# A macaron encoder block on one core: products that run on in banks filled by ScalarE, output products behind a whole group

## Chip, cores and metric

The kernel runs on one core of a Trainium2 chip. The metric is the device time of one execution in microseconds; the time of a kernel is the median of several executions. Lower is better.

## What is computed

The block takes `x` of 1024 tokens by 1024 features in float32 and applies, each with a norm in front and a residual sum behind, a half-step SwiGLU feed-forward layer, a mixing layer (a chunkwise mLSTM branch and a spatial gating branch behind one projection), and a second half-step feed-forward layer; then a last norm. All matrices are float32.

```python
def swiglu(x, w_in, w_out):                       # w_in 1024 x 5632, w_out 2816 x 1024
    gate, up = jnp.split(x @ w_in, 2, axis=-1)
    return (jax.nn.silu(gate) * up) @ w_out

x = x + 0.5 * swiglu(rmsnorm(x, ffn1_norm_g), ffn1_w_in, ffn1_w_out)
xn = rmsnorm(x, mix_norm_g)
proj = xn @ w_mix_in                              # 1024 x 8200
...                                               # mLSTM and gating branches
x = x + merged @ w_mix_out
x = x + 0.5 * swiglu(rmsnorm(x, ffn2_norm_g), ffn2_w_in, ffn2_w_out)
return rmsnorm(x, final_norm_g)
```

## The kernel before

Activations lie with features on the partitions, in two halves of 512 tokens. A float32 product is made of three products of float32r numbers: each operand is split into a rounded part (a ScalarE cast) and the rest (a VectorE subtraction), and high by high, high by low and low by high are summed in a PSUM bank of 128x512. Weights are loaded by SP into a `raw` tile (four buffers) and split into an `fw` tile (four buffers) by `unit` (L285: L287 on ScalarE, L288 on VectorE); `prod` (L291, matmul at L294) runs the products of one unit, 12 matmuls for four feature tiles, 6 for two. A framework places the instructions: each engine's queue is in order, the order comes from the framework's plan, and semaphores are set by it. Tiles of one pool are handed out in program order.

The feed-forward layer uses a scheme with seven products for a 2x2 split (gate and up columns or two output halves, two halves of the summed features, two halves of the tokens) instead of eight, with sums and differences of weights and operands.

- `first_products` (L305) runs, for all 22 feature tiles `f`, the two products of the first token half and stores two early results in DRAM (`eb`): the bank behind the first product, and the activated gate.
- `group(f)` (L321) runs the other five products for one `f`. POOL forms the weight sums (`sums`, L297: L300 to L302, and L350). The first early result is loaded into `u2` (L326). Product `t2` goes to a bank, and VectorE adds it to `u2` (L331); `t3` goes to a second bank and is added (L336); `t1` goes to a third bank `d` and is added (L341); then the function yields. Behind that the second early result is loaded (L344), `t4` is added and multiplied (L348, L349), and product `22` (L352) runs on in bank `d`, on which VectorE's L341 must have finished reading; L353 to L355 finish the gate. The hidden parts are split by `part` (L192, L193); an odd `f` forms four differences more (L365 to L371).
- `down_fast` (L381) runs the seven output products of a block of four `f` for four pairs of output tiles, with POOL's sums of 128x256 and L408, four sums from banks by VectorE (L391) and two copies by ScalarE (L397, L402) a pair; results are added to DRAM by accumulating DMAs on POOL's queue.
- `run` (L480) goes through the blocks; the output products of a block stand between the two halves of the first group of the next block. `last` (L452) finishes.

Blocks 0 to 3 have four `f` each and use `down_fast`; the last six `f` use plain output products (L430). Banks: six of `mm`, two of `ml`. The pool `t512` (11 tiles) holds `c512` tiles. In the mixing stage `feature_pair` (L148) and `token_pair` (L163) load units of four feature tiles by `load_unit` (L123). At the start eleven small DMAs on ScalarE's queue fetch parameters (L100, L104), which TensorE turns (L108) ahead of the tokens' transposes (L935).

Of the kernel before, what the change touches and what calls it, by code (L numbers as in the profile page):

```python
# [9 lines left out]
F32R = mybir.dt.float32r  # L10
# [24 lines left out]
def block_body(ctx, tc, x, ffn1_norm_g, ffn1_w_in, ffn1_w_out, mix_norm_g, w_mix_in, mlstm_conv_w,  # L35
# [31 lines left out]
    open_psum(f1, 1, mm=6, ml=2)  # L67
# [29 lines left out]
    for nm, src in (("g1", ffn1_norm_g), ("gm", mix_norm_g), ("g2", ffn2_norm_g), ("hg", mlstm_head_norm_g),  # L97
                    ("sg", sgu_norm_g), ("sb", sgu_norm_b), ("cb", mlstm_conv_b)):
        n = src.shape[-1] // P
        nc.scalar.dma_start(out=rows[at:at + n, :], in_=src[0].rearrange("(a p) -> a p", p=P))  # L100
        col[nm] = at
        at += n
    for j in range(4):
        nc.scalar.dma_start(out=rows[at:at + 16, :], in_=mlstm_conv_w[0, j].rearrange("(a p) -> a p", p=P))  # L104
# [7 lines left out]
    V.tensor_copy(out=par, in_=pt[:, 0:P])  # L112
# [10 lines left out]
    def load_unit(w_rows, ks, c0, extra=None):  # L123
# [9 lines left out]
        w = wpool[0].tile([P, 2, n, nc_], F32R, tag="w", name="w")  # L133
# [44 lines left out]
    def token_pair_wide(w_rows, c0, extra, act):  # L178
        ws = [load_unit(w_rows, ks, c0, extra) for ks in ((0, 1, 2), (3, 4, 5), (6, 7))]
# [85 lines left out]
    class Ffn:  # L265
# [31 lines left out]
        def sums(self, a11, a12, a21, a22, n):  # L297
# [23 lines left out]
        def group(self, f):  # L321
# [10 lines left out]
            w = self.unit(a21)  # L332
            b = bank("mm")
            self.prod(b, w, self.B["t3"], True, True)
            u3 = self.c512()
            V.tensor_tensor(out=u3, in0=b, in1=u2, op=ALU.add)  # L336
            w = self.unit(s1)
            d = bank("mm")
            self.prod(d, w, self.B["t1"], True, False)
            c22 = self.c512()  # L340
            V.tensor_tensor(out=c22, in0=d, in1=u3, op=ALU.add)  # L341
            yield
            sg1 = self.c512()
            nc.sync.dma_start(out=sg1, in_=self.eb[f][1])  # L344
            w = self.unit(a22)
# [28 lines left out]
            yield  # L374
# [6 lines left out]
        def down_fast(self, f0, H, acc):  # L381
            for d in range(4):
# [6 lines left out]

                def half(o, x, y):  # L390
                    V.scalar_tensor_tensor(out=o, in0=x, scalar=0.5, in1=y, op0=ALU.mult, op1=ALU.add)  # L391

# [9 lines left out]
                A.activation(out=c11, in_=a, func=AF.Copy, scale=0.5)  # L402
                G.dma_start(out=acc[0][d], in_=c11, accum_op=ALU.add)
                w = self.unit(a11, 2)
                b = bank("mm")
                self.prod(b, w, H["t2"], True, True)
                half(u2, b, u2)
                G.tensor_tensor(out=a12, in0=a12, in1=a11, op=ALU.subtract)  # L408
# [663 lines left out]
```

## Time and profile before

| | us |
|---|---|
| median of 3 runs | 2323.22 (2322.95 to 2323.43) |
| the profiled execution | 2322.64 |
| its span, first to last instruction | 2320.9 |
| TensorE busy | 2237.9 (96%) |
| VectorE busy | 1547.3 (67%) |
| ScalarE busy | 999.9 (43%) |
| GpSimd busy | 606.0 (26%) |

The profile holds one execution. PE is TensorE's matmuls, PEld its weight loads, DVE is VectorE, ACT ScalarE, POOL GpSimd, SP the engine that issues most DMAs; L294 is line 294 of the kernel. Busy is time in which an instruction ran; an engine's idle time before an instruction is put down to what ended it ("<-"). The ends of matmuls are modelled, so that a matmul is shown longer than the distance to the next one. The clock is a share of 2.4 GHz.

### The profile page before, as it was taken

How to read it: one execution, taken by the hardware profiler on the slowest of the kernel's cores; microseconds unless marked ns; L12 is line 12 of the kernel's file. 1: busy time of each engine (PE TensorE's matmuls, PEld its weight loads, DVE VectorE, ACT ScalarE, POOL GpSimd, SP SyncE). 2: the span in 40 equal slices, each digit the busy share in tenths (PEclk: the TensorE clock that was granted, in tenths of full speed). 3: DMA queues.
4: the chain of work that ended last, by engine and by line, in shares of the span. 5: the costliest groups of instructions: out<-in, count | busy, mean ns of one | idle time of the engine just before them, and what ended most of it. 6: DMA issues, size and time to landing. Idle time of an engine off the chain costs nothing. (4 is left out here: it accounts for less than half of the span.)

```text
span 2320.9 us, 30647 instructions
## 1 busy us (share of the span) xinstructions
PE 2237.9 (96%) x10979; PEld 1872.3 (81%) x10979; DVE 1547.3 (67%) x2649; ACT 999.9 (43%) x1684; POOL 606.0 (26%) x674
## 2 busy tenths in 40 slices
PE   7999999999999999999999999999999999999998
PEld 5887777777778988888889888888788777777777
DVE  6648778787467658556646575565727787877576
ACT  5633333333334345445434554543643433433333
POOL 2244545545521000000000000000215545455440
PEclk9999999999999999999999999999999999999999
DMA  8754655737753324322343353323764557366663
GB/s 264 255 176 103 142 123 124 138 106 150 159 183 123 91 81 120 100 84 81 100 146 101 89 156 91 91 82 127 251 198 145 109 136 151 93 140 126 142 181 109
DMA packets 331193, 311.52 MB, mean 134 GB/s; under 512 B 18840, under 2 KB 279576, under 8 KB 331040
## 3 DMA queue, kind: packets, MB, share of 16 engines
q1 hardware_dynamic: 292384, 217.20, 31.9%
q0 software_dynamic: 38400, 92.30, 18.7%
q8 instruction: 86, 1.41, 0.2%
q14 instruction: 67, 0.55, 0.1%
q10 hardware_dynamic: 256, 0.07, 0.0%
HBM read 223.48 MB, written 86.02 MB: 133 GB/s over the span
## 5 line engine op out<-in xcount | busy, mean ns | idle before, releaser
L294 PE MATMUL mm<-b,fw 128*128 128x512 f32 x2640 | 611.3, 392 | 23.8 <-DVE c L341 17.8
L294 PEld LDWEIGHTS mm<-b,fw 128*128 128x128 f32 x2640 | 496.2, 189 | 137.2 <-ACT fw L287 23.0
L159 PE MATMUL mm<-xn,w 128*128 128x512 f32 x2304 | 545.4, 390 | 0.0
L159 PEld LDWEIGHTS mm<-xn,w 128*128 128x128 f32 x2304 | 426.5, 188 | 82.9
L288 DVE TENSOR_TENSOR fw<-raw,fw 128x512 fp32r<-128x512 f32 (+1 forms) x472 | 325.9, 696 | 164.0 <-ACT fw L287 161.7
L294 PE MATMUL mm<-h,fw 128*128 128x512 f32 x1344 | 313.4, 393 | 21.2 <-DVE c L391 15.3
L287 ACT CAST fw<-raw 128x512 fp32r<-128x512 f32 (+1 forms) x472 | 242.3, 524 | 207.4 <-PE mm L294 133.6
L294 PEld LDWEIGHTS mm<-h,fw 128*128 128x128 f32 x1344 | 249.0, 188 | 83.9 <-issue 12.6
L135 DVE TENSOR_TENSOR w<-raw,w 128x1024 fp32r<-128x1024 f32 (+2 forms) x146 | 176.5, 1210 | 145.2 <-ACT w L134 145.0
L294 PE MATMUL mm<-xn,fw 128*128 128x512 f32 x1056 | 246.7, 395 | 4.0 <-ACT xn L192 2.1
L294 PEld LDWEIGHTS mm<-xn,fw 128*128 128x128 f32 x1056 | 199.9, 190 | 49.6 <-ACT xn L192 3.7
L134 ACT CAST w<-raw 128x1024 fp32r<-128x1024 f32 (+2 forms) x146 | 151.2, 1038 | 150.0 <-PE mm L159 82.1
L192 ACT CAST h<-c 128x512 fp32r<-128x512 f32 x136 | 82.8, 620 | 218.5 <-DVE c L349 152.1
L253 POOL DMA_DIRECT2D xs<-t x16 | 8.7, 543 | 641.4 <-DVE t L250 640.9
L300 POOL TENSOR_TENSOR s<-raw 128x512 f32<-128x512 f32 (+1 forms) x76 | 95.5, 1257 | 287.1 <-DMA raw<-in_ffn_w_in_dram 203.9
L173 PE MATMUL mm<-w,xn 128*128 128x256 f32 x1344 | 166.8, 285 | 0.2
L173 PEld LDWEIGHTS mm<-w,xn 128*128 128x128 f32 x1344 | 164.5, 193 | 1.8 <-DVE w L135 0.6
L391 DVE SCALAR_TENSOR_TENSOR c<-mm,c 128x512 f32<-128x512 f32 x160 | 110.0, 687 | 61.1 <-PE mm L294 60.8
L193 DVE TENSOR_TENSOR h<-c,h 128x512 fp32r<-128x512 f32 x136 | 100.2, 756 | 32.0 <-ACT h L192 31.6
L302 POOL TENSOR_TENSOR raw<-s,raw 128x512 f32<-128x512 f32 (+1 forms) x76 | 94.3, 1240 | 51.2 <-DVE fw L288 48.9
L448 PE MATMUL mm<-h,wl 128*128 128x512 f32 (+1 forms) x480 | 97.1, 356 | 0.0
L301 POOL TENSOR_TENSOR raw<-raw 128x512 f32<-128x512 f32 (+1 forms) x76 | 93.4, 1229 | 5.2
(244 smaller groups left out, 2548.9 us busy)
## 6 DMA issues: line engine op xcount, KB each, us to landing
raw<-in_ffn_w_in_dram SPq DMA_DIRECT2D x264, 256.0 KB, 4.2
raw<-in_w_mix_in_dram SPq DMA_DIRECT2D x124, 512.0 KB, 3.8
xd<-c POOLq DMA_DIRECT2D x160, 256.0 KB, 5.0
eb<-early POOLq DMA_DIRECT2D x88, 256.0 KB, 2.8
c<-eb SPq DMA_DIRECT2D x88, 256.0 KB, 4.6
raw<-in_ffn_w_out_dram SPq DMA_DIRECT2D x72, 256.0 KB, 3.9
xl<-xd POOLq DMA_DIRECT2D x32, 256.0 KB, 5.8
xr<-xd SPq DMA_DIRECT2D x32, 256.0 KB, 2.9
```

What stands on the lines that cost most here:

```text
L134: A.copy(out=w[:, 0, 0:n, :], in_=raw[:, 0:n, :])
L135: V.tensor_tensor(out=w[:, 1, 0:n, :], in0=raw[:, 0:n, :], in1=w[:, 0, 0:n, :].bitcast(F32), op=ALU.subtract)
L159: PE.matmul(out=banks[j], lhsT=w[:, a, i, j * P:(j + 1) * P], rhs=act[k][:, b, ts], start=(k == first and pi == 0), stop=(k == last and pi ...
L173: PE.matmul(out=o, lhsT=act[k][:, b, t * P:(t + 1) * P], rhs=w[:, a, i, :], start=(t % 2 == 0 and k == 0 and pi == 0), stop=(t % 2 == 1 an ...
L193: V.tensor_tensor(out=dst[:, 1, :], in0=src, in1=dst[:, 0, :].bitcast(F32), op=ALU.subtract)
L287: A.copy(out=w[:, 0], in_=src)
L288: V.tensor_tensor(out=w[:, 1], in0=src, in1=w[:, 0].bitcast(F32), op=ALU.subtract)
L294: PE.matmul(out=bank, lhsT=w[:, x, i, :], rhs=t[:, y, :], start=(start and i == 0 and pi == 0), stop=(stop and i == len(b) - 1 and pi == 2 ...
L300: G.tensor_tensor(out=s1, in0=a21, in1=a22, op=ALU.add)
L302: G.tensor_tensor(out=a11, in0=s1, in1=a11, op=ALU.subtract)
L391: V.scalar_tensor_tensor(out=o, in0=x, scalar=0.5, in1=y, op0=ALU.mult, op1=ALU.add)
L448: PE.matmul(out=o, lhsT=w[:, x, i, :], rhs=hs[i][:, y, ts], start=(i == 0 and pi == 0), stop=(i == n - 1 and pi == 2))
```

## The change

- In `group` the first early result is copied by ScalarE into bank `x`, in which `t2` runs on; ScalarE copies `x` into bank `y`, in which `t3` and later `t4` run on; `t1` goes to a bank of its own and is copied to `p5`. VectorE forms `y + p5` behind `t3` and `x + p5` behind `22`. The order of the products is `t2`, `t1`, `t3`, `22`, `t4`. Both early results are loaded at the group's start. The factor 0.5 goes into the hidden parts.
- `down_fast` has the same form; its weight sums are formed by VectorE instead of POOL.
- The output products of a block come behind the whole first group of the next one.
- Banks: seven of `mm`, one of `ml`. The last stage's transposes use `mm`.
- The parameter DMAs go to POOL's queue, and their transpose comes behind the tokens' (`turn_params`).
- `token_pair` loads units of three, three and two feature tiles; its split weights, and those of `token_pair_wide`, lie 16 elements into their tile.

```diff
-    open_psum(f1, 1, mm=6, ml=2)
+    open_psum(f1, 1, mm=7, ml=1)
...
-        nc.scalar.dma_start(out=rows[at:at + n, :], in_=src[0].rearrange("(a p) -> a p", p=P))
+        G.dma_start(out=rows[at:at + n, :], in_=src[0].rearrange("(a p) -> a p", p=P))
...
-    pt = psm()
-    PE.transpose(out=pt[:, 0:P], in_=rows, identity=ident)
...
+    def turn_params():
+        pt = psm()
+        PE.transpose(out=pt[:, 0:P], in_=rows, identity=ident)
+        V.tensor_copy(out=par, in_=pt[:, 0:P])
...
-        w = wpool[0].tile([P, 2, n, nc_], F32R, tag="w", name="w")
+        w = wpool[0].tile([P, 2048], F32R, tag="w", name="w")
+        w = w[:, off:off + 2 * n * nc_].rearrange("p (a k c) -> p a k c", a=2, k=n)
...
-        for u, ks in enumerate(((0, 1, 2, 3), (4, 5, 6, 7))):
-            w = load_unit(w_rows, ks, c0)
+        for u, ks in enumerate(((0, 1, 2), (3, 4, 5), (6, 7))):
+            w = load_unit(w_rows, ks, c0, off=16)
...
-            u2 = self.c512()
-            nc.sync.dma_start(out=u2, in_=self.eb[f][0])
-            s1 = self.sums(a11, a12, a21, a22, 4)
-            w = self.unit(a11)
-            b = bank("mm")
-            self.prod(b, w, self.B["t2"], True, True)
-            V.tensor_tensor(out=u2, in0=b, in1=u2, op=ALU.add)
...
-            yield
+            p1 = self.c512()
+            nc.sync.dma_start(out=p1, in_=self.eb[f][0])
             sg1 = self.c512()
             nc.sync.dma_start(out=sg1, in_=self.eb[f][1])
+            x = bank("mm")
+            A.copy(out=x, in_=p1)
+            s1 = self.sums(G, a11, a12, a21, a22, 4)
+            w = self.unit(a11)
+            self.prod(x, w, self.B["t2"], False, True)
+            y = bank("mm")
+            A.copy(out=y, in_=x)
+            w = self.unit(s1)
             b = bank("mm")
-            self.prod(b, w, self.B["t4"], True, True)
-            V.tensor_tensor(out=u3, in0=b, in1=u3, op=ALU.add)
-            V.tensor_tensor(out=u3, in0=u3, in1=sg1, op=ALU.mult)
+            self.prod(b, w, self.B["t1"], True, True)
+            p5 = self.c512()
+            A.copy(out=p5, in_=b)
+            w = self.unit(a21)
+            self.prod(y, w, self.B["t3"], False, True)
+            c22 = self.c512()
+            V.tensor_tensor(out=c22, in0=y, in1=p5, op=ALU.add)
             G.tensor_tensor(out=a12, in0=a12, in1=a11, op=ALU.subtract)
             w = self.unit(a12)
-            self.prod(d, w, self.B["22"], False, True)
-            V.tensor_tensor(out=u2, in0=d, in1=u2, op=ALU.add)
-            A.activation(out=u2, in_=u2, func=AF.Silu)
-            V.tensor_tensor(out=c22, in0=c22, in1=u2, op=ALU.mult)
+            self.prod(x, w, self.B["22"], False, True)
+            V.tensor_tensor(out=p5, in0=x, in1=p5, op=ALU.add)
+            A.activation(out=p5, in_=p5, func=AF.Silu)
+            w = self.unit(a22)
+            self.prod(y, w, self.B["t4"], False, True)
+            V.scalar_tensor_tensor(out=sg1, in0=y, scalar=0.5, in1=sg1, op0=ALU.mult, op1=ALU.mult)
+            V.scalar_tensor_tensor(out=c22, in0=c22, scalar=0.5, in1=p5, op0=ALU.mult, op1=ALU.mult)
+            u3 = sg1
...
                 w = self.unit(a11, 2)
                 a = bank("mm")
                 self.prod(a, w, H["11"], True, False)
-                u2 = self.c512()
-                A.activation(out=u2, in_=a, func=AF.Copy, scale=0.5)
-                s1 = self.sums(a11, a12, a21, a22, 2)
+                x = bank("mm")
+                A.copy(out=x, in_=a)
+                s1 = self.sums(V, a11, a12, a21, a22, 2)
+                w = self.unit(s1, 2)
+                b = bank("mm")
+                self.prod(b, w, H["t1"], True, True)
+                p5 = self.c512()
+                A.copy(out=p5, in_=b)
+                w = self.unit(a11, 2)
+                self.prod(x, w, H["t2"], False, True)
+                y = bank("mm")
+                A.copy(out=y, in_=x)
                 w = self.unit(a12, 2)
                 self.prod(a, w, H["21"], False, True)
...
                 for f in range(f0, f0 + n):
-                    g = self.group(f)
-                    next(g)
+                    self.group(f)
                     if pend is not None:
                         pend()
                         pend = None
-                    next(g)
                     spread()
...
-        bc1 = scales(0, lambda i: xt.append(turned(0, i)))
+        def step(i):
+            xt.append(turned(0, i))
+            if i == 3:
+                turn_params()
+
+        bc1 = scales(0, step)
...
-            ps = psm()
+            ps = bank("mm")
```

The rest of `down_fast` follows the same pattern: `21` in `a`, `t3` and `t4` in `y`, `22` in `x`, with VectorE's `y + p5` and `x + p5` and ScalarE's copies of `a` and the last `y`.

## Rows read from the trace of the kernel before

**Rows 1.** The page's first part: busy us, share of the span, instructions.
```profile
PE 2237.9 (96%) x10979; PEld 1872.3 (81%) x10979; DVE 1547.3 (67%) x2649; ACT 999.9 (43%) x1684; POOL 606.0 (26%) x674
```
**Rows 2.** Feed-forward stages: length, busy us of PE, PEld, DVE, ACT, POOL, clock.
```profile
153.30:661.10 507.80, 484.76 (x2090) 392.06 (x2089) 378.75 (x567) 189.32 (x372) 245.62 (x237) 0.99 0.60 133
...
1753.60:2255.70 502.10, 480.18 (x2090) 389.21 (x2088) 374.67 (x567) 189.31 (x372) 247.17 (x237) 1.00 0.60 135
```
**Rows 3.** TensorE's waits: for whom, us in total, times, longest.
```profile
PE mm L294 <- DVE c L341: 17.8, 17, 2.1
PE mm L294 <- DVE c L391: 15.3, 8, 2.1
PE mm L294 <- DVE fw L288: 7.4, 9, 1.3
PE ml L108 <- DMA raw<-in_ffn_w_in_dram: 6.5, 1, 6.5
PE mm L294 <- ACT fw L287: 6.2, 5, 1.9
```
**Rows 4.** Two groups in a row; columns as in rows 2.
```profile
266.80:280.40 13.60, 13.60 (x62) 11.26 (x61) 13.11 (x15) 4.42 (x8) 9.62 (x6) 1.00 0.63 179
280.40:295.30 14.90, 13.81 (x61) 11.15 (x60) 13.03 (x20) 6.24 (x11) 4.54 (x4) 1.00 0.27 77
```
**Rows 5.** Inside the second of them: start, us, instruction, idle time before it.
```profile
291.52 0.42 SPq L326 DMA_DIRECT2D c<-eb  x1
291.66 0.69 DVE L341 TENSOR_TENSOR c<-mm,c 128x512 f32<-128x512 f32 x1
...
292.50 4.82 PE L294 MATMUL mm<-b,fw 128*128 128x512 f32 x20 [1.08 <-DVE c L341]
...
295.65 1.62 DVE L349 TENSOR_TENSOR c<-c 128x512 f32<-128x512 f32 x1 [1.50 <-DMA c<-eb]
```
**Rows 6.** The last output pair of a block, columns as in rows 5.
```profile
252.60 3.70 DVE L288 TENSOR_TENSOR fw<-raw,fw 128x256 fp32r<-128x256 f32 x2
...
254.64 1.37 POOL L350 TENSOR_TENSOR raw<-raw 128x512 f32<-128x512 f32 x1
...
258.24 2.01 PE L294 MATMUL mm<-h,fw 128*128 128x512 f32 x6 [2.13 <-DVE c L391]
```
**Rows 7.** Groups of instructions: count, busy us, mean ns, idle before; PE whole, others first stage.
```profile
L294 PE MATMUL mm<-b,fw 128*128 128x512 f32 x2640 | 611.3, 392 | 23.8 <-DVE c L341 17.8 <-ACT fw L287 4.4 <-DVE fw L288 1.6
...
L288 DVE TENSOR_TENSOR fw<-raw,fw 128x256 fp32r<-128x256 f32 x104 | 59.5, 585 | 9.5 <-ACT fw L287 9.5
...
L336 DVE TENSOR_TENSOR c<-mm,c 128x512 f32<-128x512 f32 x22 | 15.1, 685 | 3.9 <-PE mm L294 3.9
...
L397 ACT ACTIVATE c<-mm 128x512 f32<-128x512 f32 x16 | 9.6, 597 | 12.4 <-PE mm L294 12.4
```
**Rows 8.** The page's DMA issues: count, KB each, us from issue to landing.
```profile
c<-eb SPq DMA_DIRECT2D x88, 256.0 KB, 4.6
```
**Rows 9.** Two stretches of lower clock; columns as in rows 2.
```profile
259.30:262.70 3.40, 3.40 (x10) 2.62 (x9) 1.94 (x3) 0.62 (x1) 1.73 (x2) 0.50 1.12 313
624.50:631.30 6.80, 6.20 (x13) 3.94 (x14) 6.62 (x12) 3.28 (x6) 0.00 (x0) 0.50 0.75 175
```
**Rows 10.** The start, columns as in rows 5.
```profile
8.75 0.42 ACT L903 ACTIVATE t<-xtok 128x256 f32<-128x256 f32 x1 [5.86 <-DMA t<-in_mlstm_conv_w_dram]
...
11.30 0.49 DVE L906 BATCH_NORM_STATS2 sst<-xtok 128x6 f32<-128x128 f32 x2 [0.94 <-DMA xtok<-in_x_dram]
...
25.75 24.44 PE L294 MATMUL mm<-xn,fw 128*128 128x512 f32 x94 [2.11 <-ACT xn L192]
```
**Rows 11.** Two lines: count, ns min/median/max, first and last start us.
```profile
L173 PE MATMUL mm<-w,xn x1344: 274/283/680, 727.9 to 1528.2; 128*128 128x256 f32 x192
...
L186 PE MATMUL mm<-w,xn x192: 278/285/684, 711.0 to 1217.3; 128*128 128x264 f32 x192
```
**Rows 12.** One of ScalarE's waits, columns as in rows 3.
```profile
ACT h L192 <- DVE c L349: 152.1, 44, 8.7
```

More of the change, by code (lines that the diff above doesn't have):

```diff
@@ L103, in block_body @@
     for j in range(4):
-        nc.scalar.dma_start(out=rows[at:at + 16, :], in_=mlstm_conv_w[0, j].rearrange("(a p) -> a p", p=P))
+        G.dma_start(out=rows[at:at + 16, :], in_=mlstm_conv_w[0, j].rearrange("(a p) -> a p", p=P))
         col["cw%d" % j] = at
         at += 16
-    pt = psm()
-    PE.transpose(out=pt[:, 0:P], in_=rows, identity=ident)
     par = cst.tile([P, P], F32, name="par")
@@ L111, in block_body @@
     G.memset(cpad, 0.0)
-    V.tensor_copy(out=par, in_=pt[:, 0:P])
+    def turn_params():
+        pt = psm()
+        PE.transpose(out=pt[:, 0:P], in_=rows, identity=ident)
+        V.tensor_copy(out=par, in_=pt[:, 0:P])
     def pc(nm, i):
@@ L121, in block_body, with load_unit @@
           for s in range(2)]
-    def load_unit(w_rows, ks, c0, extra=None):
+    def load_unit(w_rows, ks, c0, extra=None, off=0):
         n = len(ks)
@@ L178, in token_pair_wide @@
     def token_pair_wide(w_rows, c0, extra, act):
-        ws = [load_unit(w_rows, ks, c0, extra) for ks in ((0, 1, 2), (3, 4, 5), (6, 7))]
+        ws = [load_unit(w_rows, ks, c0, extra, 16) for ks in ((0, 1, 2), (3, 4, 5), (6, 7))]
         n = 2 * P + extra[1]
@@ L295, in prod, with sums @@
                               stop=(stop and i == len(b) - 1 and pi == 2), skip_group_check=True)
-        def sums(self, a11, a12, a21, a22, n):
+        def sums(self, G, a11, a12, a21, a22, n):
             s1 = self.sp_.tile([P, n, P], F32, tag="s", name="s")
@@ L401, in down_fast @@
                 c11 = self.c512()
-                A.activation(out=c11, in_=a, func=AF.Copy, scale=0.5)
+                A.copy(out=c11, in_=a)
                 G.dma_start(out=acc[0][d], in_=c11, accum_op=ALU.add)
[L404 to L408, printed above, removed]
-                w = self.unit(a21, 2)
-                b = bank("mm")
-                self.prod(b, w, H["t3"], True, True)
-                u3 = self.c512()
-                half(u3, b, u2)
-                w = self.unit(s1, 2)
-                e = bank("mm")
-                self.prod(e, w, H["t1"], True, False)
+                V.tensor_tensor(out=a12, in0=a12, in1=a11, op=ALU.subtract)
+                w = self.unit(a21, 2)
+                self.prod(y, w, H["t3"], False, True)
                 c22 = self.c512()
-                half(c22, e, u3)
+                V.tensor_tensor(out=c22, in0=y, in1=p5, op=ALU.add)
                 G.dma_start(out=acc[1][d + 4], in_=c22, accum_op=ALU.add)
+                w = self.unit(a12, 2)
+                self.prod(x, w, H["22"], False, True)
+                V.tensor_tensor(out=p5, in0=x, in1=p5, op=ALU.add)
+                G.dma_start(out=acc[1][d], in_=p5, accum_op=ALU.add)
                 w = self.unit(a22, 2)
-                b = bank("mm")
-                self.prod(b, w, H["t4"], True, True)
-                half(u3, b, u3)
-                G.dma_start(out=acc[0][d + 4], in_=u3, accum_op=ALU.add)
-                w = self.unit(a12, 2)
-                self.prod(e, w, H["22"], False, True)
-                half(u2, e, u2)
-                G.dma_start(out=acc[1][d], in_=u2, accum_op=ALU.add)
+                self.prod(y, w, H["t4"], False, True)
+                c21 = self.c512()
+                A.copy(out=c21, in_=y)
+                G.dma_start(out=acc[0][d + 4], in_=c21, accum_op=ALU.add)
         def down(self, f0, n, hs, acc):
@@ L439, in down @@
                         xt = self.c512()
-                        A.activation(out=xt, in_=o, func=AF.Copy, scale=0.5)
+                        A.copy(out=xt, in_=o)
                         G.dma_start(out=acc[t][d + j], in_=xt, accum_op=ALU.add)
@@ L474, in last @@
                         xt = xl[d // 2][:, d % 2, ts]
-                        V.scalar_tensor_tensor(out=xt, in0=o, scalar=0.5, in1=xt, op0=ALU.mult, op1=ALU.add)
+                        V.tensor_tensor(out=xt, in0=o, in1=xt, op=ALU.add)
                         final(t, d, part, xt)
```

24 lines of the change are left out of this document (4 added, 20 removed).

## Prediction

> **What bounds the kernel now.** I read the page's first part, then the stages, then who ends TensorE's waits, then one stretch in order of time. TensorE is busy for 96% of the span [rows 1], so only its idle time can be won, and the change keeps the number of matmuls. The two feed-forward stages hold 2090 matmuls each [rows 2]. A group without a wait has 60 of them in 13.60 us [rows 4], which is 0.2267 us apiece, so 2090 need 473.8 us. The stages took 507.8 and 502.1 us: 34.0 and 28.3 above that, 62 us together. That is the ceiling of what the feed-forward part of this change can bring.
>
> The waits name the cause. Product `22` of a group waits for VectorE's sum at L341, 17 times and 17.8 us; `22` of an output pair waits for VectorE's L391, 8 times and 15.3 us, which is once in each of the eight `down_fast`; weights that VectorE or ScalarE split late cost 7.4 and 6.2 us [rows 3]. All are products behind VectorE. A matmul is shown as 0.39 us long [rows 7] but the next follows after 0.2267, so each of these 39 waits costs 0.16 us more than shown: 46.7 + 6.4 = 53 us. Beside them the clock stood at 1.2 GHz, half, for 3.4 and 6.8 us, both times behind such a wait [rows 9]; half of 10.2 us is 5.1 us. The sum, 58, explains nearly all of the 62.
>
> Why VectorE is late is seen in [rows 4, 5]. It was busy for 13.11 us of a 13.60 us group and for 13.03 us of the next one, which took 14.90. Then it idled 1.50 us at L349 for the second early result, a DMA that SP issues late because it stands behind weight loads that themselves wait for VectorE's splits. So VectorE sets the pace there, though its share of the stage is only 379 of 508 us [rows 2].
>
> **The change part by part.**
>
> *The group.* Before, seven VectorE instructions of 128x512 read a bank or the early results: L331, L336, L341, L348, L349, L353, L355. Now there are four (`y + p5`, `x + p5`, and two products with 0.5 folded in). Three go, at 0.685 us [rows 7]: 2.05 us a group. VectorE's 13.1 us become 11.0 of 13.6. The second early result is loaded with the first, five products ahead of its use, so the 1.50 us wait goes too. The wait of `22` for L341 has a successor: product `t4` must wait until VectorE has read `y`, with `22` (12 x 0.2267 = 2.72 us) as cover, the same cover as before, but with 2 us less queued on VectorE. Of 17.8 + 17 x 0.16 = 20.5 us I let 4.5 stay: -16.
>
> *ScalarE's fills.* ScalarE gains three 128x512 copies a group. No row shows it writing a bank; the nearest is 0.597 us for bank to SBUF [rows 7]. The fills replace nothing on ScalarE, so a gain is excluded; the bounds are half and twice that row, 0.3 and 1.2, and I take 0.6. In the first feed-forward stage that is 22 x 1.8 us, and three more copies in each of 16 output pairs, 16 x 1.8: 68 us on top of 189 of 508 [rows 2], half the stage, so ScalarE does not become the bound by its sum. What counts is its order, as it takes its queue in turn. `y` is filled behind `t2` while `t1` runs (2.72 us): 0.6 us and about 0.15 us of handing over (L341 in [rows 5] starts at 291.66, takes 0.69, and TensorE starts at 292.50) leave 2 us for other work ahead of it. I put this at nothing, also at 1.2 us a fill; without that cover it costs 0.75 us a fill. Behind a waiting fill are the casts for the next weights, four buffers deep, and the splits of the hidden parts.
>
> *The seed `x`.* `t2` now cannot start before the early result has landed and been copied into its bank. In the trace the load for the next group is issued at 291.52, and that group's `t2` starts at 292.50 + 2.72 = 295.22: 3.7 us ahead [rows 5]. Such a load takes 4.6 us [rows 8], and copy and handing over another 0.75: 1.65 us late, if nothing else moved. Before, the same load was first read behind `t2`, by L331, and cost nothing. But its place behind the weight loads is set by VectorE's splits, which come earlier by the 2.05 us and the 1.50 us; then the lead is 7.2 us against 5.35 needed. At risk is every second group, the one whose load is placed while an odd group's hidden parts (L365 to L371 and five more splits) are on VectorE, as in the second of [rows 4]. For these 22 I take 0.3 us: +6.6; bounds 0 and 1.65 x 22 = 36.
>
> *The output pairs.* VectorE loses two bank sums of 0.69 us and takes over four subtractions and sums of 128x256 from POOL, at most 0.585 us each [rows 7]: +1.0 us a pair of 9.5 us (42 matmuls), hidden, as VectorE is not the bound here except once a block. POOL loses four instructions a pair. `x`, `y` and `a` are handed from product to product with one product of 6 x 0.2267 = 1.36 us between: 0.75 us is covered, 0.6 to spare. The once-a-block wait [rows 6] comes from elsewhere: POOL works on the next group's sums (1.4 us a piece), and two splits of VectorE took 3.70 us together. Those POOL sums stay, and I let half of that wait stay: of 15.3 + 8 x 0.16 = 16.6, -8.3.
>
> The Trainium skill, "SBUF — State Buffer", section "Who interferes with whom", says that a VectorE instruction with two SBUF inputs shares a port with GpSimd reads and that the later of the two is fully blocked. The 3.70 us agree with it. By that rule alone four more such instructions a pair are exposed to the sums that stay, and the half that I take off would not come; a rival below has the same from the rows.
>
> *A whole group ahead of the output products.* The block's last hidden parts now have five products instead of three to be ready, and the group's two weight buffers are free before the pairs start. That takes away most of the late splits: of 13.6 + 14 x 0.16 = 15.8 us, -10. With fewer long waits I count 3.4 of the 5.1 us of slow clock as gone.
>
> *The start.* TensorE stood 6.5 us before L108, the turning of the parameters [rows 3], and ScalarE came to its squares at 8.75 behind its own eleven DMA issues [rows 10]. The first real product started at 25.75. With the parameters behind the tokens and on POOL's queue, transposes and squares follow the tokens, whose last tile VectorE meets at 11.30 [rows 10]; from there the chain of statistics, reciprocal root, broadcast and first operand stays, 14.45 us long before, some of it VectorE's bank copies that now come earlier. POOL's eleven issues stand ahead of its stores of the turned tokens, for which nobody waits soon, and `par` is first read behind the broadcast. I take -3.5; bounds 0 and -6.5.
>
> *Nothing for the rest.* `token_pair` in three units instead of two adds one load, one cast and one split a call, in a stage without idle TensorE time. The offset of 16 elements does nothing: L186 reads its moving operand at steps of 1056 bytes, L173 at 1024, and their medians differ by 2 ns for 8 columns more [rows 11]. Seven and one banks, and 0.5 folded into the hidden parts, cost and save no measurable time. Together 0, plus or minus 3.
>
> Sum: -16 - 8.3 - 10 - 3.4 + 6.6 - 3.5 = -34.6. The profiled execution took 2322.64 us (span 2320.9), 0.6 under the median: 2288.0, and 2288.6 on the median's scale. I say 2288.
>
> **The rivals.**
>
> *Everything goes* (all 62 us and 6 at the start): 2255 to 2268. For it: VectorE is the only cause in [rows 3]. Against: each old wait has a successor.
>
> *The contention stays whole*: POOL's sums of the next group hold up VectorE in one pair a block as in [rows 6], whatever else is lighter there, so 8.3 us less are won: 2296. Against it: VectorE has two bank sums fewer in the pair, and POOL has lost its other work there.
>
> *The seeds are late* in every second group, 36 instead of 6.6 us: 2318. For it: the lead of 3.7 us. Against: what makes it short is VectorE's queue, which gets lighter.
>
> *Slower: ScalarE's queue becomes the wait.* ScalarE stood 152.1 us before the first cast of the hidden part, 44 times, 3.5 us each [rows 12]. If a fill of `y` stands behind such a cast, it comes 3.5 + 0.75 - 2.72 = 1.5 us too late in each of 44 groups: 67 us against 41 won without the seeds' cost: 2322.6 - 34.6 - 6.6 + 67 = 2348. It decides from 0.9 us a group on. Against it: that cast waited for L349, and so for the DMA that now comes early.
>
> *It doesn't do what it says* holds for the offsets alone, and is in the sum.
>
> **How the numbers follow.** Chances: forecast 0.36, 2270 to 2305; everything goes 0.14; contention 0.12; late seeds 0.15, 2305 to 2318; about no change 0.08; slower by the fills 0.15. Within 0.2% (4.6 us, about what a measurement of this kernel can tell from no change) lies the 0.08; faster is 0.36 + 0.14 + 0.12 + 0.15 = 0.77, slower 0.15. The range of 8 in 10 goes from 2256, the ceiling, to 2320, which leaves out the slower case and most of no change.
>
> **What would show it.** In the profile after: no PE wait on a VectorE sum in groups worth over 5 us; VectorE's busy time in the two stages down by some 60 us and ScalarE's up by 135; the first product before 23 us; POOL's `s` sums against VectorE in one pair a block still there. The forecast is wrong if TensorE waits for a ScalarE fill by more than 0.3 us a group, or if the loads of early results are issued under 5 us ahead of `t2`.

## The result, and the profile of the changed kernel

| | before | changed |
|---|---|---|
| median, us | 2323.32 | 2376.54 (2374.01 to 2381.86) |
| the profiled execution | 2322.64 | 2376.19 |
| its span | 2320.9 | 2374.4 |

The changed kernel is slower: 1.023 times the time of before, 95% interval 1.021 to 1.025. The forecast was 2288. The page's first part, against [rows 1]:

```profile
PE 2258.1 (95%) x10979; PEld 1881.8 (79%) x10979; DVE 1453.2 (61%) x2563; ACT 1120.8 (47%) x1924; POOL 496.7 (21%) x557
```

VectorE lost 94 us and ScalarE gained 121, as meant (97 and 122 of it in the two feed-forward stages, where the forecast had 60 and 135); TensorE has the same number of matmuls. The stretches tell where the time went: the two feed-forward stages (compare [rows 2]) and what stands behind the second one, first of the changed kernel, then the last stretch of before. Columns as in [rows 2].

```profile
152.60:673.80 521.20, 490.37 (x2090) 395.94 (x2089) 327.79 (x517) 249.91 (x486) 189.22 (x173) 0.97 0.57 129
1764.30:2287.60 523.30, 491.67 (x2090) 396.85 (x2089) 328.58 (x517) 250.40 (x486) 189.41 (x174) 0.97 0.56 130
2287.60:2374.40 86.80, 61.07 (x369) 50.05 (x367) 43.30 (x110) 19.31 (x42) 4.25 (x8) 0.95 0.23 77
```

```profile
2255.70:2320.90 65.20, 56.21 (x369) 49.23 (x367) 42.24 (x111) 19.60 (x42) 4.28 (x8) 0.95 0.33 112
```

That is +13.4, +21.2 and +21.6 us. The start gave 0.7 back (152.6 for 153.3 us) and the stretch between the two stages 2.0 (1090.5 for 1092.5): +53.5 in all, the whole difference of the two executions. TensorE's waits, against [rows 3]:

```profile
PE mm L297 <- ACT mm L333: 55.7, 18, 9.6
PE mm L1021 <- DVE xl L471: 16.8, 23, 3.2
PE ml L917 <- DVE t L914: 7.7, 1, 7.7
...
PE mm L297 <- ACT fw L290: 4.1, 6, 1.0
...
PE mm L297 <- DVE c L414: 1.9, 3, 0.6
...
PE mm L297 <- DVE fw L291: 1.2, 3, 0.4
```

The four waits that the forecast wanted to remove are gone but for 7.2 us (L290, L414, L291). Two that it put at 6.6 us and at nothing stand in their place: `t2` for the seed, which is the early result that ScalarE copies into bank `x` (L333), and the last stage's transposes (L1021) for VectorE's sum (L471). The seed, behind a block's output products, in order of time; L329 is its load, L408 one of the last pair's result copies; columns as in [rows 5]:

```profile
256.95 0.59 ACT L408 COPY c<-mm 128x512 f32<-128x512 f32 x1 [0.47 <-PE mm L297]
...
257.99 0.44 SPq L329 DMA_DIRECT2D c<-eb  x1
...
264.39 0.59 ACT L333 COPY mm<-c 128x512 f32<-128x512 f32 x1 [2.09 <-DMA c<-eb]
...
265.03 10.28 PE L297 MATMUL mm<-b,fw 128*128 128x512 f32 x37 [3.88 <-ACT mm L333]
```

The load is issued at 257.99, 3.2 us before the output pairs end (265.03 - 3.88 = 261.15). It lands 6.4 us later; ScalarE, which has stood idle for 2.09 us until then, fills the bank, and TensorE has stood for 3.88 us. Ten of the 18 waits are such ones, behind the ten groups of output products (3.88 to 9.55 us, 50.0 together); the other eight lie inside blocks, 5.7 us. Behind this wait the clock falls, here in stretches of one us:

```profile
265.00:266.00 1.00, 0.97 (x4) 0.84 (x5) 0.00 (x0) 0.00 (x0) 1.00 (x2) 1.00 1.10 293
266.00:267.00 1.00, 1.00 (x4) 0.79 (x4) 0.00 (x0) 0.00 (x0) 0.92 (x2) 0.63 1.17 276
267.00:268.00 1.00, 1.00 (x3) 0.74 (x3) 0.00 (x0) 0.00 (x0) 0.93 (x1) 0.50 1.16 229
268.00:269.00 1.00, 1.00 (x4) 0.78 (x3) 0.00 (x0) 0.00 (x0) 0.00 (x0) 0.50 1.09 214
269.00:270.00 1.00, 1.00 (x5) 0.79 (x4) 0.00 (x0) 0.46 (x1) 0.00 (x0) 0.66 0.39 68
```

The column behind POOL's is the clock: 1.2 GHz for some 3 us, which loses 0.37 + 0.5 + 0.5 + 0.34 = 1.7 us. Counted in the same way, in stretches of a quarter us while TensorE works, the other nine long waits lost 1.6 to 3.2 us each, some 22 us with this one. In seven of the ten the clock had fallen before the wait ended, as in the next block, where TensorE stands until 367.08:

```profile
362.90:365.10 2.20, 0.00 (x0) 0.00 (x0) 0.72 (x2) 1.10 (x2) 2.20 (x3) 1.00 0.97 182
365.10:367.10 2.00, 0.02 (x1) 0.02 (x1) 0.00 (x0) 0.59 (x1) 2.00 (x3) 0.54 1.12 273
367.10:372.10 5.00, 5.00 (x12) 3.95 (x13) 0.00 (x0) 0.00 (x0) 2.50 (x2) 0.50 0.95 209
```

The tail, TensorE alone:

```profile
2292.35 3.01 PE L444 MATMUL mm<-h,wl 128*128 128x512 f32 x12
2296.14 0.66 PE L1021 MATMUL mm<-ident,xl 128*128 128x128 f32 x4 [0.78 <-DVE xl L471]
2296.56 2.99 PE L444 MATMUL mm<-h,wl 128*128 128x512 f32 x12
2300.33 0.66 PE L1021 MATMUL mm<-ident,xl 128*128 128x128 f32 x4 [0.79 <-DVE xl L471]
```

Product, wait, transposes, product: nothing runs while VectorE sums. In the kernel before the transposes of one tile stood behind part of the next product:

```profile
2260.02 0.66 PE L1023 MATMUL ml<-ident,xl 128*128 128x128 f32 x4
2260.43 2.55 PE L448 MATMUL mm<-h,wl 128*128 128x512 f32 x10
2262.82 0.60 PE L1023 MATMUL ml<-ident,xl 128*128 128x128 f32 x4
```

### The profile page after: what moved, and what is told of

Its sections match the earlier page's. It is cut to its first block, busy times and chain, and to the rows that moved or that the text cites. A ratio compares the mean times of both kernels' runs of the same rounds, so it can differ in the third digit from the quotient of the medians.

```text
span 2374.4 us, 30679 instructions
## 1 busy us (share of the span) xinstructions
PE 2258.1 (95%) x10979; PEld 1881.8 (79%) x10979; DVE 1453.2 (61%) x2563; ACT 1120.8 (47%) x1924; POOL 496.7 (21%) x557
## 5 line engine op out<-in xcount | busy, mean ns | idle before, releaser
L297 PE MATMUL mm<-b,fw 128*128 128x512 f32 x2640 | 626.4, 399 | 56.7 <-ACT mm L333 55.7
L297 PEld LDWEIGHTS mm<-b,fw 128*128 128x128 f32 x2640 | 508.1, 193 | 174.6 <-ACT mm L333 64.0
L291 DVE TENSOR_TENSOR fw<-raw,fw 128x512 fp32r<-128x512 f32 (+1 forms) x472 | 316.0, 676 | 396.4 <-ACT fw L290 394.9
L297 PE MATMUL mm<-h,fw 128*128 128x512 f32 x1344 | 313.6, 393 | 5.8 <-ACT fw L290 3.1
L297 PEld LDWEIGHTS mm<-h,fw 128*128 128x128 f32 x1344 | 248.5, 188 | 69.6 <-ACT fw L290 8.2
L290 ACT CAST fw<-raw 128x512 fp32r<-128x512 f32 (+1 forms) x472 | 247.8, 526 | 101.5 <-PE mm L297 71.6
L138 DVE TENSOR_TENSOR w<-raw,w 128x1024 fp32r<-128x1024 f32 (+3 forms) x160 | 178.6, 1117 | 163.6 <-ACT w L137 163.2
L297 PE MATMUL mm<-xn,fw 128*128 128x512 f32 x1056 | 247.4, 396 | 3.6 <-ACT xn L195 2.1
L297 PEld LDWEIGHTS mm<-xn,fw 128*128 128x128 f32 x1056 | 200.5, 191 | 49.4 <-ACT xn L195 3.7
L137 ACT CAST w<-raw 128x1024 fp32r<-128x1024 f32 (+3 forms) x160 | 153.8, 963 | 178.7 <-PE mm L162 86.2
L176 PE MATMUL mm<-w,xn 128*128 128x256 f32 x1344 | 163.9, 282 | 0.0
L303 POOL TENSOR_TENSOR s<-raw 128x512 f32<-128x512 f32 x44 | 59.4, 1351 | 205.7 <-DMA raw<-in_ffn_w_in_dram 190.3
L196 DVE TENSOR_TENSOR h<-c,h 128x512 fp32r<-128x512 f32 x136 | 91.1, 689 | 5.9 <-ACT h L195 4.8
L409 POOL DMA_DIRECT2D xd<-c x32 | 28.0, 874 | 309.6 <-ACT fw L290 273.0
L444 PEld LDWEIGHTS mm<-h,wl 128*128 128x128 f32 x480 | 78.4, 192 | 12.5 <-DVE h L196 0.7
L162 PE MATMUL po<-mh,w 128*128 128x512 f32 x384 | 87.5, 389 | 0.0
```

What stands on the lines that cost most here:

```text
L137: A.copy(out=w[:, 0, 0:n, :], in_=raw[:, 0:n, :])
L138: V.tensor_tensor(out=w[:, 1, 0:n, :], in0=raw[:, 0:n, :], in1=w[:, 0, 0:n, :].bitcast(F32), op=ALU.subtract)
L162: PE.matmul(out=banks[j], lhsT=w[:, a, i, j * P:(j + 1) * P], rhs=act[k][:, b, ts], start=(k == first and pi == 0), stop=(k == last and pi ...
L176: PE.matmul(out=o, lhsT=act[k][:, b, t * P:(t + 1) * P], rhs=w[:, a, i, :], start=(t % 2 == 0 and k == 0 and pi == 0), stop=(t % 2 == 1 an ...
L196: V.tensor_tensor(out=dst[:, 1, :], in0=src, in1=dst[:, 0, :].bitcast(F32), op=ALU.subtract)
L290: A.copy(out=w[:, 0], in_=src)
```

## The experiments

Theory: both losses have one cause, the order in which a pool's tiles are handed out. `p1` comes from the pool of 128x512 results, so its tile, and with it its load, comes behind the 16 result tiles of the output products. The transposes' bank comes from `mm`, so the bank of the next output tile comes behind transposes that wait for VectorE. The rivals: slow transfers, ScalarE's queue, SP's queue, and the split of the banks into seven and one. Where a run adds lines, its line numbers move: L298 is the changed kernel's L297, and so on; what a moved line does is said beside it.

### The transposes' bank

```diff
-            ps = bank("mm")
+            ps = psm()
```

> The changed kernel, with one edit: the last stage's transposes (L1021) write the small bank `ml` again, of which there is now one. Theory: in `mm` their bank stands between those of two output tiles, and as the banks of a pool are handed out in program order the next output tile's product cannot be placed ahead of transposes that wait for VectorE's sum L471; with `ml` it can. Then the 23 waits of TensorE for L471 (16.8 us) nearly go, the stretch from the last stage's first product to the end falls from 86.8 to about 66 us, and the time from 2376.5 to about 2356. Rival: the single small bank is itself the cause (seven and one instead of six and two); then the waits turn into waits of the transposes for VectorE's product that reads the bank, and the time stays within 5 us of 2376.5.

2354.09 us (1.014 of before, 1.012 to 1.017), 22.4 less; the stretch behind the second stage took 65.0 us and 0.5 us of waits for L471 is left. The rival was then tried by itself, with the transposes left in `mm`:

```diff
-    open_psum(f1, 1, mm=7, ml=1)
+    open_psum(f1, 1, mm=6, ml=2)
...
-        open_psum(f2, 3, mm=7, ml=1)
+        open_psum(f2, 3, mm=6, ml=2)
```

> The changed kernel, with one edit: the banks are shared six and two again (`mm`, `ml`), while the last stage's transposes stay in `mm`. Theory (handing out in order within `mm`): the transposes still stand right behind each sum, about 23 waits for L471 with 16 to 17 us remain, the time from the last stage's first product to the end stays at 84 to 88 us, the time at 2370 to 2382. Rival (seven and one): the waits go and the time falls to about 2355.

2379.88 us, and the same 23 waits with 16.8 us. The pool is the cause, not the number of banks.

### The seed

```diff
+            self.ep = pool("ep", 2)
...
-            p1 = self.c512()
+            p1 = self.ep.tile([P, NH], F32, tag="early", name="p1")
...
-TMP = 11
+TMP = 9
```

> The changed kernel, with one edit: the first early result `p1`, from which ScalarE fills bank `x`, comes from a pool of its own with two tiles; the other results of 128x512 have 9 tiles instead of 11. Theory: `p1` was loaded late because its tile is handed out behind the 16 result tiles of the output pairs; now its load stands about a group earlier on SP's queue. TensorE's wait for L333 (55.7 us, 18 times) falls below 5 us, the slow clock behind these waits goes with it, the two feed-forward stages fall from 521.2 and 523.3 to 482 to 487 us each, and the time from 2376.5 to about 2300. Rival: the transfer itself is slow (6.4 to 8.4 us behind the output pairs) or the fill is late on ScalarE's queue: then more than 30 us of the wait stay and the time is above 2340.

2303.67 us (0.992 of before, 0.989 to 0.994), 72.9 less than the changed kernel, though the tail's loss is still in it. The stages took 488.3 and 483.4 us, and no wait for the seed is left. The load (L330 here), the fill (L334) and the first product behind the output products (L298):

```profile
199.64 0.44 SPq L330 DMA_DIRECT2D p<-eb  x1
```
```profile
254.55 0.59 ACT L334 COPY mm<-p 128x512 f32<-128x512 f32 x1
```
```profile
259.16 3.13 PE L298 MATMUL mm<-b,fw 128*128 128x512 f32 x13
```

The load now goes out ahead of the output products and the bank is full 4 us ahead of its product. Was it SP's queue, where weight loads wait for buffers?

```diff
-            nc.sync.dma_start(out=p1, in_=self.eb[f][0])
+            nc.scalar.dma_start(out=p1, in_=self.eb[f][0])
```

> The changed kernel, with one edit: the load of `p1` is issued on ScalarE's queue instead of SP's; the tile still comes from the shared pool. Theory (the tile is handed out behind the output pairs' result tiles): the load is issued no earlier than the last pair's last result copy, so the waits for L333 stay above 50 us, and the time is between 2370 and 2400. Rival (SP's queue, where the load stands behind weight loads that wait for buffers, is the cause): the load goes out by 4 us or more earlier, the wait falls below 20 us and the time to 2320 or less.

2391.79 us; the wait grew to 69.7 us. On ScalarE's queue the load stands right behind the last pair's last result copy, the 16th of the 16 tiles, so that a queue without weight loads did not bring it forward:

```profile
260.94 0.58 ACT L423 COPY c<-mm 128x512 f32<-128x512 f32 x1 [0.90 <-PE mm L297]
261.00 0.40 ACTq L329 DMA_DIRECT2D c<-eb  x1
...
267.13 0.59 ACT L333 COPY mm<-c 128x512 f32<-128x512 f32 x1 [5.03 <-DMA c<-eb]
```

To part the order from the pool's size, the tile was left in the shared pool and only asked for earlier; the transposes are in `ml` here:

```diff
                     if pend is not None:
+                        self.ahead[f + 1] = self.early(f + 1)
                         pend()
```

> The changed kernel with the last stage's transposes in `ml` (as tail_psm), and one edit more: the first early result of the group behind the output products is asked for and loaded ahead of them in program order; it stays in the shared pool of eleven tiles. Theory (what made it late is its place behind the output pairs' result tiles in the order in which one pool's tiles are handed out, and not the number of tiles or the pool): the ten long waits for L333 (50 us) and the slow clock behind them go, the short ones inside a block stay with some 5 us; 2354 minus 65 to 72 makes 2282 to 2289, a few us above pool_tail. Rival (a pool of its own was what helped): waits for L333 stay above 30 us, time above 2325.

2299.58 us: 54.5 less than with the transposes alone. The long waits went and 7.6 us of short ones stayed, so the order is the cause. But the time missed the expected 2282 to 2289, for a wait that I had not foreseen (here L338 fills the seed `x` and L343 fills `y`):

```profile
PE mm L298 <- ACT mm L343: 10.9, 8, 2.6
PE mm L298 <- ACT mm L338: 7.6, 8, 2.5
```

One of the eight, on ScalarE and then on TensorE:

```profile
273.82 0.59 ACT L338 COPY mm<-c 128x512 f32<-128x512 f32 x1 [4.14 <-DMA c<-eb]
274.34 0.61 ACT L291 CAST fw<-raw 128x512 fp32r<-128x512 f32 x1
...
279.93 2.33 ACT L195 CAST h<-c 128x512 fp32r<-128x512 f32 x4 [3.93 <-DVE c L374]
282.17 0.58 ACT L343 COPY mm<-mm 128x512 f32<-128x512 f32 x1
```
```profile
282.80 1.53 PE L298 MATMUL mm<-b,fw 128*128 128x512 f32 x4 [2.60 <-ACT mm L343]
```

The seed of a later group, whose load is still late, holds ScalarE for 4.14 us; VectorE waits for the cast behind it, the hidden parts' casts wait for VectorE, and the fill of `y` comes behind them. This is the forecast's slower rival, in its mechanism: a fill of `y` behind a cast that waits for VectorE.

### Two ways to cover the seed

```diff
+            w = self.unit(s1)
+            b = bank("mm")
+            self.prod(b, w, self.B["t1"], True, True)
+            p5 = self.c512()
+            A.copy(out=p5, in_=b)
             w = self.unit(a11)
             self.prod(x, w, self.B["t2"], False, True)
             y = bank("mm")
             A.copy(out=y, in_=x)
-            w = self.unit(s1)
...
```

> The changed kernel, with one edit: in each group product `t1`, which needs no filled bank, runs ahead of `t2`. Theory: the early result lands when it landed before, but the seed has one product of 12 matmuls (2.72 us) more as cover. The ten long waits behind output products (3.9 to 9.6 us, 50 us together) lose 2.72 us each, the eight short ones (5.7 us together) go: 55.7 to about 23 us, time about 2343, or down to 2325 if the slow clock behind the long waits goes too. Rival, something other than the landing of the early result ends the wait (ScalarE's order): the wait stays above 45 us and the time above 2365.

The wait for the seed fell to 21.0 us, as expected, but the time stayed at 2377.93: `t3`, which runs in `y`, now follows `t2` with no product between, and waits for the fill (L343 here):

```profile
PE mm L297 <- ACT mm L343: 36.3, 42, 2.2
PE mm L297 <- ACT mm L333: 21.0, 10, 4.9
```

That is the price of a fill without cover: 36.3 / 42 = 0.86 us shown, 1.02 with the 0.16 of a wait that the forecast worked out; it had supposed 0.75.

The output products were put back into the middle of the group, with a `yield` between `t3` and `22`:

```diff
             V.tensor_tensor(out=c22, in0=y, in1=p5, op=ALU.add)
+            yield
...
                 H["t4"].append(self.part(bigp, u3))
+            yield
...
-                    self.group(f)
+                    g = self.group(f)
+                    next(g)
                     if pend is not None:
                         pend()
                         pend = None
+                    next(g)
```

> The changed kernel, with one edit: the output products of a block stand in the middle of the next block's first group again, between `t3` and `22`, instead of behind the whole group. Theory: the next group's early result still comes behind the output pairs' tiles, but two products (5.44 us) stand between the pairs and `t2`: of the ten long waits for L333 only the two longest keep 1.5 and 4.1 us, the wait falls from 55.7 to below 12 us, and the time to between 2300 and 2320 (late splits of hidden parts, which the whole group was to cover, may give back up to 10 us). Rival: the place of the output products does nothing to the seeds: wait above 45 us, time above 2365.

2360.51 us, and the wait still 49.0: a miss. Two products more stand between the pairs and the next group, but the seeds are still late, by 1.74 and 3.97 us behind the first two blocks. In the first the load went out at 254.55 as the pairs ended, where it had gone out 3 us ahead of their end; it moved along with the weight loads ahead of it on SP. Two products, 5.44 us, are less than the 6.6 us that this load took (to 261.18) and its fill. Why the ten loads behind output products take 6.1 to 8.5 us in the changed kernel, against a median of 4.3 on the page, was not tried; while the one shown was under way, from 257.99 to 264.39, the DMA engines' busy share was 0.96.

### The rest of the change, with both losses mended

The edits of tail_psm and seed_pool together:

```diff
-            p1 = self.c512()
+            p1 = self.ep.tile([P, NH], F32, tag="early", name="p1")
...
-            ps = bank("mm")
+            ps = psm()
```

> The changed kernel with both edits together: `p1` from a pool of its own (two tiles, nine instead of eleven for the rest), and the last stage's transposes in `ml`. Theory: the two losses are separate, 72.9 and 22.4 us of 2376.5 in the runs of each alone; together about 2281, and about 40 us under the kernel before, which is the size that the forecast gave to the rest of the change. Rival: they overlap (the end of the second feed-forward stage is delayed into the tail in both), then 2290 or more.

2279.64 us, 0.981 of before (0.979 to 0.983): faster than both kernels, and the two losses add. The stages and the tail:

```profile
152.31:636.04 483.73, 478.84 (x2089) 389.69 (x2088) 346.61 (x516) 250.66 (x486) 193.22 (x175) 1.00 0.60 138
1726.18:2209.22 483.04, 478.85 (x2090) 389.74 (x2089) 349.37 (x516) 250.91 (x486) 192.65 (x172) 1.00 0.60 140
2209.22:2275.10 65.88, 56.05 (x369) 49.03 (x367) 41.82 (x110) 18.82 (x42) 4.25 (x8) 0.93 0.31 101
```

Of the 62 us above 473.8 a stage, 9.9 + 9.2 are left, at a clock of 1.00. From here single parts were undone. The place of the output products, by the edit of mid:

```diff
+            yield
```

> As pool_tail (both losses mended), and the output products in the middle of the next block's first group again. The forecast gave 10 us to the place behind a whole group (late splits of hidden parts and of weights): then this is about 10 us slower than pool_tail, 2291, and TensorE waits for hidden parts (L195, L196) or split weights at the first product of the pairs. Rival: VectorE has so much less to do that the splits are in time at either place; then it is within 3 us of pool_tail.

2293.20 us, 13.6 more: the size is as forecast, the way is not. The waits that return are for the fill of `y` (11.3 us, 9 times, the longest 3.9), and the longest stands behind hidden parts' casts on ScalarE as in ahead_tail.

The sums of an output pair on GpSimd:

```diff
-                s1 = self.sums(V, a11, a12, a21, a22, 2)
+                s1 = self.sums(G, a11, a12, a21, a22, 2)
...
-                V.tensor_tensor(out=a12, in0=a12, in1=a11, op=ALU.subtract)
+                G.tensor_tensor(out=a12, in0=a12, in1=a11, op=ALU.subtract)
```

> As pool_tail, and the four weight sums of each output pair are formed by GpSimd again instead of VectorE. Theory: what ended the once-a-block wait of product `22` (15.3 us in the kernel before) was VectorE being slowed by GpSimd's sums and queued behind its own bank sums; with GpSimd's work back in the pairs, VectorE's 128x256 splits get longer again (585 ns against about 430) and waits of 1 to 2 us a block return: 5 to 10 us slower than pool_tail. Rival: the filled banks alone took the wait away; then within 3 us of pool_tail.

2292.26 us, 12.6 more, again by another way than expected. VectorE's splits of 128x256 took 593 ns on average against 573, hardly longer. TensorE waits for ScalarE's fill of `y` in the pairs (L405), and ScalarE for GpSimd: the cast ahead of the fill needs a difference (L411) that stands behind the next group's sums in GpSimd's queue:

```profile
PE mm L298 <- ACT mm L405: 13.6, 8, 3.2
```
```profile
ACT fw L291 <- POOL raw L411: 27.1, 16, 4.4
```

In pool_tail VectorE forms that difference. It takes 0.43 us at the median, and 2.04 in the pair where GpSimd works on the next group's sums, so the slowing of [rows 6] is still there; but TensorE now waits only 0.62 to 0.64 us behind it, once in each of the eight `down_fast`, and 0.2 more in three of them:

```profile
241.76 2.04 DVE L411 TENSOR_TENSOR raw<-raw 128x256 f32<-128x256 f32 x1
241.94 1.57 POOL L305 TENSOR_TENSOR raw<-raw 128x512 f32<-128x512 f32 x1
```

The banks, six and two:

```diff
-    open_psum(f1, 1, mm=7, ml=1)
+    open_psum(f1, 1, mm=6, ml=2)
...
-        open_psum(f2, 3, mm=7, ml=1)
+        open_psum(f2, 3, mm=6, ml=2)
```

> As pool_tail (`p1` from its own pool, transposes in `ml`), with six banks in `mm` and two in `ml`. The forecast put seven and one at no cost and no gain: then within 3 us of pool_tail, 2277 to 2283. Rival: the filled banks need the seventh (`x`, `y`, `b` of one group beside those of the next): then fills and products wait for a bank, and it is 5 us or more slower.

2280.26 us (2273.28 to 2289.84), no difference from 2279.64 that these runs can tell: the split of the banks costs nothing measurable, as forecast.

The offset of 16 elements, taken back:

```diff
-            w = load_unit(w_rows, ks, c0, off=16)
+            w = load_unit(w_rows, ks, c0, off=0)
...
-        ws = [load_unit(w_rows, ks, c0, extra, 16) for ks in ((0, 1, 2), (3, 4, 5), (6, 7))]
+        ws = [load_unit(w_rows, ks, c0, extra, 0) for ks in ((0, 1, 2), (3, 4, 5), (6, 7))]
```

> As pool_tail, with the split weights of `token_pair` and `token_pair_wide` at the start of their tile again (offset 0), units of three, three and two kept. In the changed kernel and in b_units the matmuls of `token_pair` followed each other after 118 ns (median), in the kernel before after 120. If the offset does that: 120 again, and 1344 x 2 ns = 2.7 us more in the stage. Rival (the finer units do it): 118 stays.

96 matmuls of `token_pair` in a row, with the offset and then without it:

```profile
764.32 11.47 PE L176 MATMUL mm<-w,xn 128*128 128x256 f32 x96
```
```profile
763.50 11.68 PE L176 MATMUL mm<-w,xn 128*128 128x256 f32 x96
```

The kernel before has 11.68 for 96 too. The offset does it: 0.21 x 14 such runs = 2.9 us. (All 1344 are shown busy for 166.8 us in the kernel before and for 163.9 in b_units, which has the offset.) The time, 2280.86, can't tell so little.

Two parts were put into the kernel before, alone. The start:

```diff
-        nc.scalar.dma_start(out=rows[at:at + n, :], in_=src[0].rearrange("(a p) -> a p", p=P))
+        G.dma_start(out=rows[at:at + n, :], in_=src[0].rearrange("(a p) -> a p", p=P))
...
+            if i == 3:
+                turn_params()
```

> The kernel before, with the start of the changed kernel alone (parameter loads on GpSimd's queue, their transpose behind the tokens'). The forecast gave -3.5 us, bounds 0 and -6.5. In the changed kernel the first product came at 24.41 us instead of 25.75, and its wait before it was for the chain of statistics: so -1 to -2 us here, first product between 24.0 and 24.8. Rival: -3.5, first product before 23.

The first product came at 23.39 us instead of 25.75, earlier than the expected 24.0 to 24.8; the ratio is 1.000 (0.999 to 1.002). In the profiles of the changed kernel and of its variants it came between 23.27 and 24.76, in b_units, which has the start of before, at 25.26. So a gain of 1 to 2 us is in the traces and too small for the times.

And the units and the offset of the mixing stage:

```diff
-        w = wpool[0].tile([P, 2, n, nc_], F32R, tag="w", name="w")
+        w = wpool[0].tile([P, 2048], F32R, tag="w", name="w")
+        w = w[:, off:off + 2 * n * nc_].rearrange("p (a k c) -> p a k c", a=2, k=n)
...
-        for u, ks in enumerate(((0, 1, 2, 3), (4, 5, 6, 7))):
-            w = load_unit(w_rows, ks, c0)
+        for u, ks in enumerate(((0, 1, 2), (3, 4, 5), (6, 7))):
+            w = load_unit(w_rows, ks, c0, off=16)
...
```

> The kernel before, with the units of three, three and two tiles and the offset of 16 elements in `token_pair` and `token_pair_wide` alone. The forecast gave 0, plus or minus 3: stage from the first output product of the last group before it to the second feed-forward stage within 3 us of the 983.3 us before. Rival: finer units bring each product's weights earlier and the stage is 2 us shorter, as between the two kernels (981.3).

2317.02 us, 0.998 of before (0.996 to 0.999). The stretch took 978.6 us; in b_start, which has the same mixing stage as before, it took 981.4, in the kernel before 983.3. So 3 to 5 us are won, of which the offset explains 2.9.

## Why the prediction was wrong

*The seed.* This is the step that failed. "In the trace the load for the next group is issued at 291.52": the lead of 3.7 us was read inside a block and taken for all 22 groups at risk, with 1.65 x 22 = 36 us as the upper bound. Inside blocks the sum came near, 5.7 + 8 x 0.16 = 7.0 us against 6.6 forecast, by luck in its terms: eight waits of 0.7 us instead of 22 of 0.3, and a lead of 4.3 to 4.5 us where 7.2 was expected. But ten groups stand behind output products, and the bound did not hold for them: 50.0 + 10 x 0.16 = 51.6 us, and the 22 us of slow clock. The forecast's own sign, loads under 5 us ahead of `t2`, was met: the load shown went out 3.2 us ahead, and behind the plain output products the loads went out only as these ended (624.36 against 624.08). The trace of before had it, in its first block:

```profile
258.03 0.42 SPq L326 DMA_DIRECT2D c<-eb  x1
...
260.05 1.48 PE L294 MATMUL mm<-b,fw 128*128 128x512 f32 x3
```

The load went out 2 us before the output products ended. That cost nothing, since the first reader, L331, came behind two products of the group in progress and behind `t2`: 3 x 2.72 us later. The change took away all three: the seed is read ahead of `t2`, and the whole group stands ahead of the output products. By this row, with the forecast's 4.6 us for the load and 0.75 for the fill, the seed would have been 3.3 us late (258.03 + 4.6 + 0.75 = 263.38 against 260.05); with the landing of 6.4 us that the changed kernel shows, 5 us (258.03 + 6.4 + 0.7 = 265.1). I counted "a whole group ahead" as a gain only, and did not ask which loads it uncovers. I also wrote that the load's place behind the weight loads is set by VectorE's splits. The weight loads ahead of it do wait for these splits, but what put it behind them was the order in which the pool's tiles are handed out, as seed_pool, ahead_tail and eb_act show.

*The tail.* "Seven and one banks ... cost and save no measurable time" is right of the number (pool_tail_62) and wrong of the edit beside it: that the last stage's transposes use `mm` was not weighed at all. It cost 21.6 us.

*What was right.* Group, output pairs, whole group and clock were put at -16 - 8.3 - 10 - 3.4 = -37.7. With the seeds mended the 62.3 us fell to 19.1, by 43.2. The once-a-block wait in the pairs, of which half was to stay, fell from 15.3 us shown to 5.0: eight waits of 0.61 to 0.64, three for VectorE's sum L414 and five for a cast (L290). That is -10.3 with the 0.16 of each, for the -8.3 forecast. By the Trainium skill's "SBUF — State Buffer", "Who interferes with whom", the half should have stayed, by that rule alone. The trace agrees in that VectorE is held up beside GpSimd's sums (0.43 us against 2.04 for the difference above) and that one wait a block stays, a third of the old ones. What GpSimd's sums in the pairs cost on top came through ScalarE's queue (pool_tail_gsums), where the splits on VectorE differ by 20 ns on average. The place of the output products was worth 13.6 instead of 10, through late fills of `y` and not late splits, so that the size was luck. A fill takes 570 to 590 ns where 0.6 us was supposed. The mended kernel's 2279.64 lies in the forecast's own range of 2270 to 2305, but it is not the kernel that was forecast.

*The start* gave 1.3 us at the first product (24.41 for 25.75; the sign asked for under 23), and 0.7 at the first product of the groups, where -3.5 was put. The wait moved from L108 to the chain of statistics (L917, 7.7 us), which begins with the last token tile: VectorE meets that at 11.67 where it was 11.30. So the tokens did not come earlier, and the gain is the chain behind them, 12.74 us long where it was 14.45. The sum was taken from what stood first in the queue, and the tokens' own landing stood right behind it.

*The rest*, 0 plus or minus 3, measured -2.0; but "the offset of 16 elements does nothing" is wrong. I compared the displayed lengths of two lines of different shape [rows 11], and not the distances of one shape.

*The rivals.* "The seeds are late" was the right one and had its price from the wrong place, 36 us instead of 76 (58.6 of waits and 17 of clock). "ScalarE's queue becomes the wait" was not what happened in the changed kernel (its fill of `y`, L338, was waited for twice, 0.8 us), but ahead_tail, pool_tail_mid and pool_tail_gsums each brought it out: 11 to 14 us of waits for a fill late on ScalarE's queue. Put together: the waits for seeds are +58.6 and the clock +17 (22 lost where the kernel before lost 5). The two stages are 34.6 longer, which leaves -41 for the groups and pairs, near the 43.2 of pool_tail, in which 5 are clock. With +21.6 in the tail, -0.7 and -2.0 that makes +53.5.

## What to carry to other kernels

When an edit moves a first read forward or moves work ahead of other work, take each load that was covered by the moved part and read its issue and landing at every kind of place, above all behind the stretch with the most tiles in flight; one lead from the middle of the pattern is no bound. Where tiles of a pool are handed out in order, a tile whose first write waits must not share a pool with tiles that others need at once: give it a pool of its own. An engine that takes its queue in order passes one late operand on to all that stand behind it, so count for each fill what stands ahead of it.

## What the hardware showed beside

The distance of matmuls with 256 columns of moving operand depended on where the operand begins: 11.68 us for 96 with the split weights at the start of their tile, 11.47 with 16 elements (64 bytes) of offset, in the same program otherwise. And the clock fell at no fixed place behind TensorE's waits: with a wait of 4.19 us it fell to 0.50 some 1.9 us before the wait ended, with one of 4.21 us (it ends at 2081.26) some 0.8 us behind its end.
